# Layer 0's softmax-attention gate: weights stationary, a pair of row tiles moving

## The chip, the cores and the metric

The kernel runs on one core of a Trainium2 chip, in one launch. The core has TensorE (PE, with its weight loads shown apart as PEld), VectorE (DVE), ScalarE (ACT), GpSimd (POOL) and SyncE (SP, which issues DMAs). The metric is the device time of the kernel in microseconds (us), lower is better, as a median over several runs.

## The reference

A flow-matching backbone of two layers over 2304 tokens (256 of context, 2048 latent) of width 1024. Layer 0 mixes with multi-head latent attention and gated linear attention side by side, layer 1 with neighbourhood attention. Cut to the gate that the change concerns, which is `za` (512 features, `lat[3]` and `cp[3]`):

```
lat = split_cols(jnp.dot(h, w_in), EVEN_SPLITS)
...
a_x = block_attention(q_x, jnp.concatenate([k_x, k_c], axis=1), jnp.concatenate([v_x, v_c], axis=1), scale)
...
a = a.reshape(bsz, n, A_WIDTH) * jax.nn.silu(za)
b = rms_norm(b, gla_gain).reshape(bsz, n, B_WIDTH).astype(zb.dtype) * jax.nn.silu(zb)
return jnp.dot(jnp.concatenate([a, b], axis=-1), w_out)
```

`h` is the normed and modulated input of the layer, `zb` the like gate of the linear attention. SiLU is computed as (tanh(z/2) + 1) * z, a factor of 2 being taken care of elsewhere.

## The kernel before

Tokens are cut into 18 row tiles (NT) of 128 (P); the width of 1024 into 8 chunks (KD) of 128. Each float32 product is made of three matmuls over rounded halves: high by high, high by low and low by high (`mm3_steps`, lines L129, L130 and L131).

The stage concerned is `even_rest`. It projects the part of layer 0's input projection that is left over, 2080 columns in five pieces (`REST`): j = 0 is the gate `za` (512 columns, its weights called WU), j = 1 the gate `zb` (512, wr1), and j = 2, 3, 4 are three pieces of 352 (W0, W1, W2) for the linear attention. One `cell(t, j)` makes one piece for one row tile: 24 matmuls with a token tile (hhi or hlo, 128 x 128) stationary and the weights moving, into one of two PSUM banks called gm; tokens come out on the partitions. Both gates then take a tanh on ACT and a multiply on DVE (L632) into u, whose result POOL's queue sends to a scratch in DRAM. The gate `za` is wanted with its features on the partitions, since the attention reads it that way (`azt`, L966); so with j = 0 TensorE also transposes u in four blocks of 128 x 128 (L638) into a PSUM bank of its own, tp, ACT copies that to zt, and POOL sends zt to `zaT` (L641).

`stream` walks the cells in an order made by `cells`: per row tile the pieces 2, 3, 4, 0, 1, with two tiles taken together at either end. Pieces 2 and 3 of tiles 16 and 17 are made elsewhere, so there are 86 cells. It holds two token tiles (`hbufs`); after a tile's last cell `reload` fetches another: a DMA on SP's queue into x (one buffer), an ACT copy that makes hhi and a DVE subtraction that makes hlo.

`weave` puts a second sequence in between, `maxes`: for each of 8 heads it makes the scores of all queries (matmuls of 96 x 512, some of 96 x 256, into one of five PSUM banks mx, L665), of which DVE takes the row maximum (L666). At a head's end `post` transposes the 18 columns of maxima (L675), ACT copies them (mr), and POOL sends them into the queries' scratch (QT, L678). Besides, `weave` splits weights ahead of their use (`pump`), wr1 among them: a DMA into wraw, an ACT copy (L106 is the helper of all ACT work) and a DVE subtraction (L387).

Behind the stage comes `even_attention`. It first sets one row of each of four key buffers to one (memsets of akh on POOL, L910), loads queries and keys, and makes scores (st, L1016 to L1018) whose exponentials ACT takes (apt). Loading ACT's table for them is L1043.

Each engine takes its instructions in the order in which a scheduler has put them when the program is built; the order written in the code is where it starts from.

Of the kernel before, what the change touches and what calls it, by code (L numbers as in the profile page):

```python
# [11 lines left out]
F32R = mybir.dt.float32r  # L12
AF = mybir.ActivationFunctionType
ALU = mybir.AluOpType
# [3 lines left out]
P = 128  # L18
D = 1024
KD = D // P  # L20
# [3 lines left out]
NT = T // P  # L24
# [64 lines left out]
class Kern:  # L89
# [86 lines left out]
    def cells(tiles, js, keep=lambda t, j: True, edge=2):  # L176
# [2 lines left out]
        groups = [tiles[:edge]] + [[t] for t in tiles[edge : n - edge]] + [tiles[n - edge :]]  # L179
        return [(t, j) for g in groups for j in js for t in g if keep(t, j)]  # L180

    def stream(self, cells, hT, cell, prep, done=None):

        last = {}
        for n, (t, j) in enumerate(cells):
            last["t", t] = last["j", j] = n
        tiles = list(dict.fromkeys(t for t, _ in cells))
        for t in tiles[: self.hbufs]:
            if t not in hT:
                hT[t] = prep(t)  # L190
        for n, (t, j) in enumerate(cells):
            yield from cell(t, j)
            if last["j", j] == n and done:
                done(j)
            if last["t", t] == n:
                i = tiles.index(t) + self.hbufs
                if i < len(tiles):
                    del hT[t]
                    hT[tiles[i]] = prep(tiles[i])

    def rpow(self, out, in_, mul, add):
# [112 lines left out]
    def prep_pool(self, es, name, side, bufs, wbufs):  # L314
        self.prp = self.pool(es, name, bufs=2, side=side, reuse_waits="tile")
        self.hbufs, self.wbufs = bufs, wbufs

    def prep(self, l, t, src, pp, tag):

        return self.modulate(l, t, *self.transposed(t, src, pp, tag))  # L320

    def transposed(self, t, src, pp, tag, xp=None):

        nc, sp = self.nc, self.prp
        x = self.tl(xp or sp, [P, D], "x", bufs=1)
# [4 lines left out]
        self.act(lo[:].rearrange("p k t -> p (k t)"), x[:], AF.Square, accum_out=ss[:, 0:1])  # L330
# [21 lines left out]
    def reload(self, l, t):  # L352

        nc, sp = self.nc, self.prp
        x = self.tl(sp, [P, D], "x", bufs=1)
        nc.sync.dma_start(x[:], self.H[l, t])
        h = x[:].rearrange("p (k t) -> p k t", k=KD)
        hi = self.tl(sp, [P, KD, P], "hhi", F32R, bufs=self.hbufs)
        lo = self.tl(sp, [P, KD, P], "hlo", F32R, bufs=self.hbufs)
        self.act(hi[:], h)  # L360
        nc.vector.tensor_tensor(out=lo[:], in0=h, in1=hi[:], op=ALU.subtract)
        return hi, lo

    def split_w(self, *a, **kw):
# [248 lines left out]
    def even_rest(self, ws, win, hT):  # L613
        nc = self.nc
        self.zaT = self.scr("zaT", (4, P, T), F32)
        with ExitStack() as es:
            wp = self.pool(es, "ewB", side="left", reuse_waits="tile")
            sp = self.pool(es, "esB", bufs=2, side="left", reuse_waits="tile")
            pp = self.pool(es, "epB", bufs=2, space=PSUM, reuse_waits="tile")
            self.ahead += [self.rest_steps(win, 0, ws, "WU"), self.rest_steps(win, 1, wp, "wr1")]  # L620

            def cell(t, j):
                hi, lo = hT[t]
# [6 lines left out]
                if j < 2:  # L630
                    self.last_tanh = self.act(u[:], ps[:], AF.Tanh, scale=0.5)
                    nc.vector.scalar_tensor_tensor(out=u[:], in0=u[:], scalar=1.0, in1=ps[:], op0=ALU.add, op1=ALU.mult)  # L632
                else:
                    self.act(u[:, :w], ps[:, :w])
                if j == 0:
                    pt = self.tl(pp, [P, 4, P], "tp", bufs=1)
                    for b in range(4):
                        nc.tensor.transpose(pt[:, b, :], u[:, b * P : b * P + P], self.ident[:])  # L638
# [3 lines left out]
                elif j == 1:  # L642
                    nc.gpsimd.dma_start(self.Un[t, :, 1056:], u[:])
                else:
                    nc.gpsimd.dma_start(self.Un[t, :, (j - 2) * 352 : (j - 1) * 352], u[:, :352])

            cells = self.cells(list(range(NT))[::-1], (2, 3, 4, 0, 1), lambda t, j: j not in (2, 3) or t < NT - 2)
            gemms = self.stream(cells, hT, cell, lambda t: self.reload(0, t))

            def maxes():  # L650
                post = None
                for h in range(A_HEADS):
                    k = self.tl(sp, [P, T], "mk", F32R, bufs=2)
                    nc.sync.dma_start(k[:A_QK].bitcast(F32), self.KT[h, 0, :A_QK])
                    m = self.tl(sp, [P, NT, 5], "mm")
                    nc.vector.memset(m[:], -3e38)
                    for t in range(NT):
                        if t % 6 == 0:
                            q = self.tl(sp, [P, 768], "mq", F32R)
                            nc.sync.dma_start(q[:A_QK].bitcast(F32), self.QT[h, 0, :A_QK, t * P : t * P + 768])  # L660
                        lim = CTX if t < NCT else T
                        for n, k0 in enumerate(range(0, lim, 512)):
                            w = min(512, lim - k0)
                            ps = self.tl(pp, [P, 512], "mx", bufs=5)
                            mm = nc.tensor.matmul(ps[:, :w], q[:A_QK, (t % 6) * P : (t % 6) * P + P], k[:A_QK, k0 : k0 + w], start=True, stop=True)  # L665
                            nc.vector.tensor_reduce(out=m[:, t, n : n + 1], in_=ps[:, :w], axis=AX.X, op=ALU.max)  # L666
                            yield mm
                        if t == 3 and post:
                            yield post()
                    mc = self.tl(sp, [P, NT], "mc", bufs=1)  # L670
                    nc.vector.tensor_reduce(out=mc[:], in_=m[:], axis=AX.X, op=ALU.max)

                    def post(h=h, mc=mc):
                        ps = self.tl(pp, [P, 512], "mx", bufs=5)
                        mm = nc.tensor.transpose(ps[:NT, :P], mc[:], self.ident[:])  # L675
                        r = self.tl(sp, [P, P], "mr", F32R, bufs=1)
                        self.act(r[:NT], ps[:NT, :P], AF.Copy, scale=-1.0)
                        nc.gpsimd.dma_start(self.QT[h, 0, A_QK].rearrange("(t p) -> t p", p=P), r[:NT].bitcast(F32))  # L678
# [673 lines left out]
    def gate(self, out, in_):  # L1352

        self.last_tanh = self.act(out[:], in_, AF.Tanh, scale=0.5)
        self.nc.vector.scalar_tensor_tensor(out=out[:], in0=out[:], scalar=1.0, in1=in_, op0=ALU.add, op1=ALU.mult)
# [526 lines left out]
```

## Time and profile before

| | |
|---|---|
| runs shown | 3616.67, 3619.09, 3619.68 us; median 3619.09 |
| the profiled execution: own time | 3617.2 us |
| its span | 3615.4 us |
| the gate stage's steady part in the trace | 561.56 to 1083.06 us |

The span is what the profiler saw of the program's instructions; the own time has what lies around it. Views of the trace name a group as line, operation and tiles: `gm<-wr1h,hhi` is a matmul that writes gm from wr1's high half and a token tile's high half. Shapes stand as partitions x elements. "idle before" with an arrow says how long the engine stood before the instruction, and what released it.

### The profile page before, as it was taken

The page shows a single profiled execution, that of the slowest core. Times are in us where ns is not written, and L with a number is a line of the kernel's source. Part 1 is how long each engine was busy: PE and PEld are TensorE (multiplying, and loading weights), DVE is VectorE, ACT ScalarE, POOL GpSimd, SP SyncE. Part 2 cuts the span into 40 slices and gives each one's busy share as a digit, 9 for nine tenths or more (in the row PEclk, how much of TensorE's full clock was granted, in tenths as well). Part 3 has the DMA queues.
Part 4 walks back from the last instruction along what each step waited for, and adds up shares of the span by engine and source line. Part 5 has one row for each costly group of instructions (what it writes and reads, how often), then busy time and mean ns, then how long its engine had stood idle before and what let it go on. Part 6 is the DMA issues. An engine that isn't in the chain of part 4 may idle for free. (4 is left out here: it accounts for less than half of the span.)

```text
span 3615.4 us, 51630 instructions
## 1 busy us (share of the span) xinstructions
PE 3523.6 (97%) x18260; PEld 2734.3 (76%) x18260; DVE 2372.3 (66%) x4876; ACT 1430.5 (40%) x2705; POOL 1212.6 (34%) x1342
## 2 busy tenths in 40 slices
PE   8999999999999999999999999999999999999899
PEld 6988998888886666656667878888788886555577
DVE  4677665888886776787664345444587874667721
ACT  5544551111115555555653134444422223555510
POOL 1433430111011232212312233333334444677743
PEclk9999999999999999999999999999999999999999
DMA  7555463222233343334534544456643437888654
GB/s 253 149 153 159 141 191 99 87 77 84 75 109 89 83 104 83 94 92 129 163 91 143 162 164 127 145 143 199 212 139 123 139 122 202 213 213 222 185 178 146
DMA packets 396683, 513.62 MB, mean 142 GB/s; under 512 B 61229, under 2 KB 275197, under 8 KB 390522
## 3 DMA queue, kind: packets, MB, share of 16 engines
q1 hardware_dynamic: 353242, 418.68, 40.0%
q0 software_dynamic: 20192, 56.97, 5.6%
q10 hardware_dynamic: 22992, 34.68, 2.8%
q8 instruction: 145, 2.38, 0.3%
q14 instruction: 112, 0.92, 0.1%
HBM read 330.61 MB, written 179.59 MB: 141 GB/s over the span
## 5 line engine op out<-in xcount | busy, mean ns | idle before, releaser
L1007 DVE TENSOR_TENSOR acc<-acc,apt 128x512 f32<-128x512 f32 x512 | 376.4, 764 | 150.6 <-ACT apt L106 147.0
L666 DVE TENSOR_REDUCE mm<-mx 128x1 f32<-128x512 f32 (+1 forms) x656 | 392.7, 627 | 90.6 <-PE mx L665 82.3
L106 ACT ACTIVATE apt<-st 128x512 f32<-128x512 f32 (+1 forms) x592 | 342.9, 593 | 269.0 <-PE st L1018 229.5
L958 PE MATMUL av<-apt,av 128*64 128x512 f32 (+1 forms) x1184 | 269.2, 592 | 0.0
L1016 PE MATMUL st<-aq,akh 97*128 97x512 f32 x576 | 246.8, 428 | 0.2 <-ACT apt L106 0.2
L665 PE MATMUL mx<-mk,mq 96*128 96x512 f32 (+1 forms) x656 | 238.5, 372 | 0.0
L1017 PE MATMUL st<-aq,akh 96*128 96x512 f32 x576 | 229.1, 398 | 0.0
L1018 PE MATMUL st<-aq,akl 96*128 96x512 f32 x576 | 228.5, 397 | 0.0
L1450 DVE CUSTOM_DVE_ANT_1 mx<-mx,mtab 128x465 f32<-128x465 f32 (+14 forms) x576 | 183.9, 338 | 47.2 <-PE mx L1444 34.5
L106 ACT ACTIVATE u<-gm 128x352 f32<-128x352 f32 (+1 forms) x144 | 70.3, 495 | 358.5 <-PE gm L131 207.7
L106 ACT ACTIVATE opt<-opt 128x930 f32<-128x930 f32 (+9 forms) x144 | 119.2, 830 | 234.5 <-POOL opt L1748 137.0
L958 PEld LDWEIGHTS av<-apt,av 128*64 128x64 f32 x1184 | 79.9, 137 | 152.0 <-issue 150.0
L1708 DVE TENSOR_TENSOR opt<-st,tab 128x64 f32<-128x64 f32 (+10 forms) x576 | 143.0, 314 | 78.3 <-PE st L1548 44.7
L1583 POOL TENSOR_TENSOR oacc<-oacc,opt 128x682 f32<-128x682 f32 (+9 forms) x144 | 173.9, 1230 | 37.8 <-ACT opt L106 36.6
L1016 PEld LDWEIGHTS st<-aq,akh 97*128 97x128 f32 x576 | 109.0, 189 | 72.7 <-issue 44.2
L665 PEld LDWEIGHTS mx<-mk,mq 96*128 96x128 f32 x656 | 122.7, 188 | 11.7
L1018 PEld LDWEIGHTS st<-aq,akl 96*128 96x128 f32 x576 | 110.2, 191 | 25.5
L1017 PEld LDWEIGHTS st<-aq,akh 96*128 96x128 f32 x576 | 110.6, 192 | 17.8
L106 ACT ACTIVATE x<-px,modB,modA 128x128 f32<-128x128 f32 x272 | 99.1, 468 | 58.5 <-PE px L335 39.5
L1547 PE MATMUL st<-q,kt 128*128 128x480 f32 (+5 forms) x256 | 98.7, 388 | 20.2 <-DVE opt L1708 14.8
L129 PE MATMUL gm<-w0h,hhi 128*128 128x512 f32 x288 | 115.3, 400 | 2.3 <-DVE hhi L347 2.3
L129 PE MATMUL gm<-w1h,hhi 128*128 128x512 f32 x288 | 116.7, 405 | 0.0
(584 smaller groups left out, 9906.5 us busy)
## 6 DMA issues: line engine op xcount, KB each, us to landing
q<-Q SPq DMA_DIRECT2D x48, 512.0 KB
H<-x ACTq DMA_DIRECT2D x36, 512.0 KB
adaw<-ada_w SPq DMA_DIRECT2D x64, 256.0 KB
x<-H SPq DMA_DIRECT2D x32, 512.0 KB
K1t<-okt POOLq DMA_DIRECT2D x32, 512.0 KB, 6.7
kt<-K1t SPq DMA_DIRECT2D x32, 512.0 KB
mtab<-rpb_q SPq DMA_DIRECT2D x16, 899.0 KB
QT<-qkhl SPq DMA_DIRECT2D x36, 384.0 KB
```

The costliest lines, as they stand in the source:

```text
L106: return self.nc.scalar.activation(out, in_, func, **kw)
L129: self.nc.tensor.matmul(out, lh(k), rh(k), start=j == 0, stop=False)
L665: mm = nc.tensor.matmul(ps[:, :w], q[:A_QK, (t % 6) * P : (t % 6) * P + P], k[:A_QK, k0 : k0 + w], start=True, stop=True)
L666: nc.vector.tensor_reduce(out=m[:, t, n : n + 1], in_=ps[:, :w], axis=AX.X, op=ALU.max)
L958: nc.tensor.matmul(O[j, nb][i * 64 : i * 64 + 64, :w], V[j, kt // TT][:, kt % TT, i * 64 : i * 64 + 64], pts[i][:, :w], start=n == 0, stop ...
L1007: self.add = nc.vector.tensor_tensor(out=acc[i][:, :w], in0=a[:, :w], in1=pts[i][:, :w], op=ALU.add)
L1016: nc.tensor.matmul(ps[:, :w], kh[: A_QK + 1, i, kq], qh[: A_QK + 1, :w], start=True, stop=False)
L1017: nc.tensor.matmul(ps[:, :w], kh[:A_QK, i, kq], ql[:A_QK, :w], start=False, stop=False)
L1018: mm = nc.tensor.matmul(ps[:, :w], kl[:A_QK, i, kq], qh[:A_QK, :w], start=False, stop=True)
L1450: nc.vector.tensor_tensor_reduce(out=s, in0=s, in1=tb[:, ri : ri + rn, ci : ci + cn], scale=1.0, scalar=-3e38, op0=ALU.add, op1=ALU.max, a ...
L1583: self.psum = nc.gpsimd.tensor_tensor(out=a, in0=a, in1=pts[:, :, a0 - r0 : a1 - r0, :], op=ALU.add)
L1708: nc.vector.tensor_tensor(out=pt[:, d[0], d[1]], in0=ps[:, d[0], d[1]], in1=tabs[j][i][:, ri : ri + rn, ci : ci + cn], op=ALU.add)
```

## The change

The gate `za` is made for a pair of row tiles at once by `pair_steps`. Stationary is a slice of 128 of the weights' columns, that is 128 features; moving are the two tiles side by side, 256 tokens. To lay them side by side, the two token tiles now sit in one ring tile per half, `[P, bufs, KD, P]`, and a tile's place in it is `t % hbufs` (`slots`). A pair makes two blocks; each fills one gm bank with two groups of 128 features by 256 tokens, in 48 matmuls, with a step of the weave after each 6. The features come out on the partitions, tanh and multiply run on the block as it is, and POOL sends u to `zaT` without a transpose. There are 864 matmuls of 256 columns where there were 432 of 512; the columns streamed are the same. The 72 transposes, the 18 ACT copies and the bank tp are gone; mx has six banks in place of five. The multiplies and the sends to `zaT` stay 18 each.

The order of cells is written out: for a pair (t, t + 1) the pieces 2, 3, 4, 1 of tile t + 1, the gate of both, then 2, 3, 4, 1 of tile t, with the first and last pair apart.

```
+    def pair_steps(self, ps, blk, w):
+        hi, lo = self.ring
+        wh, wl = w
+        for n in range(2):
+            c = slice((blk + n) * P, (blk + n) * P + P)
+            o = ps[:, n * 256 : n * 256 + 256].rearrange("p (a t) -> p a t", a=2)
+            for j, k in enumerate(range(KD)):
+                self.nc.tensor.matmul(o, wh(k)[:, c], hi[:, :, k, :], start=j == 0, stop=False)
+                self.nc.tensor.matmul(o, wh(k)[:, c], lo[:, :, k, :], start=False, stop=False)
+                mm = self.nc.tensor.matmul(o, wl(k)[:, c], hi[:, :, k, :], start=False, stop=j == KD - 1)
+                if j % 2:
+                    yield mm
...
+        self.ring = [self.tl(self.prp, [P, bufs, KD, P], "h" + z, F32R, bufs=1) for z in ("hi", "lo")]
+    def slots(self, t):
+        return [r[:, t % self.hbufs] for r in self.ring]
...
-        hi = self.tl(sp, [P, KD, P], "hhi", F32R, bufs=self.hbufs)
-        lo = self.tl(sp, [P, KD, P], "hlo", F32R, bufs=self.hbufs)
+        hi, lo = self.slots(t)
...
+            def gated(t, j):
+                wh, wl = win[j]
+                for b in (0, 2):
+                    ps = self.tl(pp, [P, 512], "gm")
+                    yield from self.pair_steps(ps, b, (lambda k: wh[:, k, :], lambda k: wl[:, k, :]))
+                    u = self.tl(sp, [P, 512], "u", bufs=4)
+                    gate(u, ps)
+                    nc.gpsimd.dma_start(self.zaT[b : b + 2, :, t[0] * P : t[0] * P + 256].rearrange("j p t -> p j t"),
+                                        u[:].rearrange("p (j t) -> p j t", j=2))
...
-                if j == 0:
-                    pt = self.tl(pp, [P, 4, P], "tp", bufs=1)
-                    for b in range(4):
-                        nc.tensor.transpose(pt[:, b, :], u[:, b * P : b * P + P], self.ident[:])
-                    z = self.tl(sp, [P, 4, P], "zt")
-                    self.act(z[:], pt[:])
-                    nc.gpsimd.dma_start(self.zaT[:, :, t * P : t * P + P].rearrange("j p t -> p j t"), z[:])
...
+            cells = []
+            for t in range(NT - 2, -1, -2):
+                both = (t, t + 1)
+                if t == NT - 2:
+                    cells += [(t + 1, 4), (t, 4), (both, 0), (t + 1, 1), (t, 1)]
+                elif t == 0:
+                    cells += [(x, j) for j in (2, 3, 4) for x in (1, 0)] + [(both, 0), (1, 1), (0, 1)]
                 else:
-            cells = self.cells(list(range(NT))[::-1], (2, 3, 4, 0, 1), lambda t, j: j not in (2, 3) or t < NT - 2)
+                    cells += [(t + 1, j) for j in (2, 3, 4, 1)] + [(both, 0)] + [(t, j) for j in (2, 3, 4, 1)]
...
-                            ps = self.tl(pp, [P, 512], "mx", bufs=5)
+                            ps = self.tl(pp, [P, 512], "mx", bufs=6)
```

`stream` is taught that a cell may belong to two tiles. Lines of the changed program are shifted: the three matmuls of `pair_steps` are L190, L191 and L192, the maxima's matmuls L699, their transpose L709 and its send L712, the memsets L944, the first scores L1050.

On PE, in the middle of the stage, the transposes of a gate cell stand between the matmuls of the wr1 cell that follows (numbers behind a name count buffers). Before:

```order
L129 MATMUL gm_6485<-wr1h_5766,hhi_5963 128x512
L130 MATMUL gm_6485<-wr1l_5767,hhi_5963 128x512
L638 MATMUL tp_6477<-ident_58,u_6474 128x128 x2
L665 MATMUL mx_6332<-mk_5847,mq_6207 128x256
L638 MATMUL tp_6477<-ident_58,u_6474 128x128
L665 MATMUL mx_6338<-mk_5847,mq_6207 128x512
L638 MATMUL tp_6477<-ident_58,u_6474 128x128
```

With the change the gate's matmuls are 256 wide, and name the ring tile first and the weights second:

```order
L190 MATMUL gm_6262<-hhi_87,WUh_5658 128x256
L191 MATMUL gm_6262<-hlo_88,WUh_5658 128x256
L699 MATMUL mx_6228<-mk_5847,mq_6205 128x512
L192 MATMUL gm_6262<-hhi_87,WUl_5659 128x256
L190 MATMUL gm_6262<-hhi_87,WUh_5658 128x256
L191 MATMUL gm_6262<-hlo_88,WUh_5658 128x256
L699 MATMUL mx_6237<-mk_5847,mq_6205 128x256
L192 MATMUL gm_6262<-hhi_87,WUl_5659 128x256
```

No transposes are left there; score matmuls stand between the narrow ones as they stood between the wide ones.

On PE, at the end of the stage, the last head's maxima are transposed shortly before the last wr1 matmuls and the first scores. Before:

```order
L665 MATMUL mx_10352<-mk_9808,mq_10166 128x256
L129 MATMUL gm_10456<-wr1h_5766,hhi_10015 128x512
L130 MATMUL gm_10456<-wr1l_5767,hhi_10015 128x512
L131 MATMUL gm_10456<-wr1h_5766,hlo_10016 128x512
L675 MATMUL mx_10360<-ident_58,mc_10358 18x128
L129 MATMUL gm_10456<-wr1h_5766,hhi_10015 128x512
L130 MATMUL gm_10456<-wr1l_5767,hhi_10015 128x512
L131 MATMUL gm_10456<-wr1h_5766,hlo_10016 128x512
L1016 MATMUL st_12158<-aqc_10517,akh_1874_10509 128x256
```

With the change, from the same transpose (L709) on; the three rows from L130 to L129 stand there four times in all before two more follow:

```order
L129 MATMUL gm_10696<-wr1h_5744,hhi_87 128x512
L709 MATMUL mx_10575<-ident_58,mc_10573 18x128
L130 MATMUL gm_10696<-wr1l_5745,hhi_87 128x512
L131 MATMUL gm_10696<-wr1h_5744,hlo_88 128x512
L129 MATMUL gm_10696<-wr1h_5744,hhi_87 128x512
L130 MATMUL gm_10696<-wr1l_5745,hhi_87 128x512
L131 MATMUL gm_10696<-wr1h_5744,hlo_88 128x512
L129 MATMUL gm_10696<-wr1h_5744,hhi_87 128x512
```

Behind the transpose stood 3 wr1 matmuls, and now 14 stand there ahead of the first score matmul.

On POOL, at the same place, with what each instruction waits for, the order stays: the send of the maxima, then the memsets. With the change:

```order
L712 DMA QT<-mr_10577 18x128 [waits DMASW4_49,Activation_49]
L944 MEMSET akh_1772_10749 1x1536 [waits PE_49,Pool_49]
L944 MEMSET akh_1773_10750 1x1536
L944 MEMSET akh_1774_10751 1x1536
L944 MEMSET akh_1775_10752 1x1536 [waits PE_49]
```

Before, the same five stood there as L678 and L910; the memsets come behind the send on POOL, and so behind the maxima's copy on ACT. Moved is only the place of the transpose on PE that this send goes back to.

More of the change, by code (lines that the diff above doesn't have):

```diff
@@ L194, in stream @@
                 done(j)
[L195 to L198, printed above, removed]
+            for x in of(t):
+                i = tiles.index(x) + self.hbufs
+                if last["t", x] == n and i < len(tiles):
+                    del hT[x]
                     hT[tiles[i]] = prep(tiles[i])
@@ L357, in reload @@
         h = x[:].rearrange("p (k t) -> p k t", k=KD)
[L358 to L361, printed above, removed]
+        hi, lo = self.slots(t)
+        self.act(hi, h)
+        nc.vector.tensor_tensor(out=lo, in0=h, in1=hi, op=ALU.subtract)
         return hi, lo
@@ L673, in post @@
                     def post(h=h, mc=mc):
-                        ps = self.tl(pp, [P, 512], "mx", bufs=5)
+                        ps = self.tl(pp, [P, 512], "mx", bufs=6)
                         mm = nc.tensor.transpose(ps[:NT, :P], mc[:], self.ident[:])
```

26 lines of the change are left out of this document (16 added, 10 removed).

## The prediction

> **What bounds the kernel now.** I read the totals first, then the chain of waits, then the stage that the change touches.
>
> ```profile
> span 3615.4 us, 51630 instructions
> PE 3523.6 (97%) x18260; PEld 2734.3 (76%) x18260; DVE 2372.3 (66%) x4876; ACT 1430.5 (40%) x2705; POOL 1212.6 (34%) x1342
> PE 40%; DVE 2%; DMA 1%; issue 1%; ACT 1%; POOL 0%; SPq 0%; POOLq 0%; DVEq 0%; ACTq 0%
> ```
>
> TensorE is busy for 97% of the span, and the chain of work that ended last runs over it and hardly over anything else. The next view cuts out the gate stage (its steady part, then its end), the stretch behind it, and one later stretch for comparison. The columns are: stretch, length, busy time of PE, PEld, DVE, ACT and POOL, granted clock, DMA share, GB/s.
>
> ```profile
> core 0: us, PE busy (x) PEld busy (x) DVE busy (x) ACT busy (x) POOL busy (x), PEclk, DMA share, GB/s
> 561.56:1083.06 521.50, 521.40 (x2700) 462.07 (x2698) 429.61 (x721) 69.67 (x123) 52.51 (x90) 1.00 0.28 84
> 1083.06:1086.26 3.20, 1.32 (x10) 1.14 (x9) 0.69 (x1) 1.88 (x3) 3.11 (x3) 1.00 0.57 148
> 1086.69:1093.40 6.71, 6.71 (x17) 5.42 (x18) 1.54 (x3) 3.22 (x7) 3.15 (x5) 0.51 1.07 244
> 2872.70:2876.00 3.30, 3.04 (x15) 2.41 (x16) 3.30 (x13) 1.82 (x3) 0.26 (x1) 1.00 0.70 238
> ```
>
> In the steady part PE is busy 521.40 of 521.50 us at full clock: every matmul microsecond added or taken away there is a microsecond of the kernel. DVE is second with 429.61 (82%). ACT and POOL have far more room (70 and 53). At the end of the stage PE works 1.32 of 3.20 us, and behind it runs at half the clock.
>
> **Transposes that go.** The matmul timeline around one gate cell's transposes (start, length, then what; lengths overlap, so I read differences of starts):
>
> ```profile
> 727.12 0.39 PE L129 MATMUL gm<-wr1h,hhi 128*128 128x512 f32 x1
> ...
> 728.74 0.60 PE L638 MATMUL tp<-ident,u 128*128 128x128 f32 x4
> 729.10 0.48 PE L665 MATMUL mx<-mk,mq 96*128 96x512 f32 x1
> 729.42 0.40 PE L129 MATMUL gm<-wr1h,hhi 128*128 128x512 f32 x1
> L638 PE MATMUL tp<-ident,u x72: 270/272/475, 560.8 to 1073.5; 128*128 128x128 f32 x72
> ```
>
> Seven 512-wide matmuls take 727.12 to 728.74, 1.62 us, so 0.2314 each, with a weight load between each two. The four transposes take 0.36, and the matmul behind them 0.32 instead of 0.23: 0.45 us for one tile. There are 72 transposes, so 18 such groups: 18 x 0.45 = **-8.1 us**. The 18 ACT copies out of tp and their PSUM bank go too; ACT has room, so that is worth nothing, and a sixth mx bank is no gain where PE never waits.
>
> **Width.** The gate had 18 tiles x 8 chunks x 3 = 432 matmuls of 512 columns. Now there are 9 pairs x 4 feature groups x 8 x 3 = 864 of 256: the same columns, with 432 more weight loads. No pair of 128-row tiles ran that way before, so I look for 256-wide matmuls that each follow a load of their own. The nearest are the score matmuls right behind the stage, and around them the ends:
>
> ```profile
> 1085.34 0.28 PE L1017 MATMUL st<-aqc,akh 96*128 96x256 f32 x1
> 1085.46 0.28 PE L1016 MATMUL st<-aqc,akh 97*128 97x256 f32 x1
> 1085.46 0.19 PEld L1017 LDWEIGHTS st<-aqc,akh 96*128 96x128 f32 x1
> 1085.94 0.52 PE L1018 MATMUL st<-aqc,akl 96*128 96x256 f32 x3
> ...
> 2603.32 0.40 PE L1437 MATMUL mx<-mk,mz 128*128 128x256 f32 x2
> 2603.55 0.40 PE L131 MATMUL gm<-w0h,hlo 128*128 128x512 f32 x1
> ...
> 1081.16 0.29 PE L665 MATMUL mx<-mk,mq 96*128 96x256 f32 x1
> 1081.29 0.39 PE L129 MATMUL gm<-wr1h,hhi 128*128 128x512 f32 x1
> ...
> 1155.14 1.06 PE L791 MATMUL gl<-gu,gat 128*128 128x128 f32 x8
> 1155.95 0.47 PE L1017 MATMUL st<-aq,akh 96*128 96x512 f32 x1
> ```
>
> From 1085.34 to 1085.94 five steps take 0.60, so 0.120 each, though the load record alone is 0.19: loads run under the matmul ahead. The low end is the pair at 2603.32, 0.23 for two (0.115); the high end the lone one at 1081.16, 0.13. I take 0.120, since it is the row with a new weight at each step. 864 x 0.120 = 103.7 against 432 x 0.2314 = 100.0: **+3.7 us** (at 0.115 it is -0.6, at 0.13 it is +12.3). Eight 128-wide matmuls, each with its load, pass in 0.81, 0.101 each; below that a load could not be hidden, and 256 columns stay above it.
>
> [...]
>
> **The start of the stage.** Its first gate cell's ending is held up by weight splitting:
>
> ```profile
> 557.83 1.06 ACT L106 ACTIVATE wr1h<-wraw 128x1024 fp32r<-128x1024 f32 x1 [12.28 <-DMA wraw<-w_rest]
> 558.79 0.58 ACT L106 ACTIVATE u<-gm 128x512 f32<-128x512 f32 x1
> 560.06 0.68 DVE L632 SCALAR_TENSOR_TENSOR u<-u,gm 128x512 f32<-128x512 f32 x1
> 560.79 1.12 PE L638 MATMUL tp<-ident,u 128*128 128x128 f32 x4 [4.33 <-DVE u L632]
> 561.56 0.78 PE L129 MATMUL gm<-wr1h,hhi 128*128 128x512 f32 x1
> ```
>
> ACT stands at the split of a wr1 piece until its DMA lands; the tanh waits behind it, the multiply (L632) behind that, and PE waits 4.33 us. Without transposes the next PE work is the wr1 cell, which needs a gm bank that the same multiply gives back and the same wr1 pieces. So the stall stays: 0 (at best -0.8, the 0.77 us of these transposes, of which 0.45 is counted above).
>
> **The end of the stage.** What lies around the last matmul:
>
> ```profile
> 1082.24 0.28 PE L675 MATMUL mx<-ident,mc 128*18 128x128 f32 x1
> 1082.83 0.40 PE L131 MATMUL gm<-wr1h,hlo 128*128 128x512 f32 x1
> 1083.12 0.53 POOL L678 DMA_DIRECT2D QT<-mr  x1 [5.07 <-PE gm L130]
> 1083.32 0.60 ACT L106 ACTIVATE u<-gm 128x512 f32<-128x512 f32 x1 [0.49 <-PE gm L131]
> 1083.68 4.00 POOL L910 MEMSET akh<- 1x1536 f32 x3
> 1083.93 1.28 ACT L1043 ACT_TABLE_LOAD   x1
> 1085.11 0.39 PE L1016 MATMUL st<-aqc,akh 97*128 97x256 f32 x1 [1.88 <-POOL akh L910]
> 1086.26 0.38 ACT L106 ACTIVATE apt<-st 128x256 f32<-128x256 f32 x1 [1.04 <-PE st L1018]
> ```
>
> The last head's maxima are transposed (L675), copied, and sent by POOL; behind that issue stand POOL's memsets, and the first of them (4.00/3 = 1.33 us) holds the first score matmul for 1.88 us. From L675 to that memset's end it is 1083.68 + 1.33 - 1082.24 = 2.77 us. In the new order 14 wide matmuls follow that transpose instead of 3: 14 x 0.2314 = 3.24 us, so the memset is done before PE is, and PE may start 1085.11 - 1083.06 = 2.05 earlier. Late next is ACT: its tanh (1083.32) and the table load end at 1085.21, and no exponential can start before, where now it starts at 1086.26. **-1.0 us** (ends 0 and -2.05). Should the max's ending come late again, the 1.0 is lost.
>
> **The slow clock behind it.**
>
> ```profile
> 1087.50 0.63 PE L1016 MATMUL st<-aq,akh 97*128 97x512 f32 x1
> 1093.40 0.39 PE L1018 MATMUL st<-aq,akl 96*128 96x512 f32 x1
> ...
> 2872.70 0.66 PE L1395 MATMUL tp<-ident,ovz 128*128 128x128 f32 x4 [1.66 <-DVE ovz L1355]
> ```
>
> Fourteen matmuls take 1087.50 to 1093.40, 5.90 us, against 14 x 0.2314 = 3.24 at full clock: 2.66 lost. PE had idled 1.88 and soon after 1086.69 - 1086.26 = 0.43. In the new order PE works on until its score banks are full and waits for ACT, by my count 1.3 us. After an idle of 1.66 us (2872.70) the window above shows clock 1.00. I take **-2.7** (the other end is 0, the drop stays).
>
> [...]
>
> **Covers.** DVE's multiplies keep their number; the 18 sends to zaT also. The cell order now runs four or five cells of one token tile in a row, and the other tile's reload (a copy, a subtraction and a DMA) has to be done before the pair cell. The 86 cells of the old order share some 521 us, 6.1 each with the maxima between them, so four cells give 24 us; a reload is a DMA, and a copy and a subtraction of the size of the wr1 rows above (1.06 and 1.22), so it is hidden. Uncovered, it would show as PE waiting for DVE at L191 for each pair.
>
> **Sum**, against the profiled execution (span 3615.4, 3617.2 with what lies around it): -8.1 + 3.7 - 1.0 - 2.7 = -8.1, so 3609.1. The median of the runs shown lies 1.9 above it, at 3619.09: forecast **3611**.
>
> **Rivals.**
>
> *The load sets the pitch of a narrow matmul* (slower). In a long run of 256-wide matmuls the loads could fail to keep ahead: the record of one is 0.19. Then 864 x 0.19 = 164.2, +64.2 - 11.8 (the other three terms) = +52, some 3671. It decides from a pitch of 0.125 on, where width (108.0 - 100.0) eats the transposes; at 0.133 the whole is nil. For it: five steps are a short chain, and PEld's work in this stage grows from 462 by 432 x 0.19 = 82 to 544, beyond 521. Against it: records overlap, and the 0.101 of eight in a row. Chance 0.15.
>
> *The end term or the clock does not come*: the idle keeps its length, the clock falls as it did, and transposes less width remain, -4.4, 3615: within what can be told from no change. For it: my count of 1.3 us idle lies close to the 1.88 that went wrong. Chance 0.22.
>
> *DVE becomes the bound in bursts.* DVE has 82% now, and a stretch where maxima (one per wide score matmul) come close together can make PE wait for an mx bank. If each of 18 gate ends costs 0.3, less than half of an L632 multiply of 0.68, 5.4 us go, -2.7 in all, 3616. Against it: six banks instead of five. Chance 0.08.
>
> *The change does not overlap as written*: the pair cell waits for both tiles, and one reload is late in each of 9 pairs by more than 0.9 us: no gain, 3619 or more. Chance 0.05.
>
> **The numbers.** The forecast has 0.50. What a measurement of this kernel can tell from no change is about 0.2%, 7.2 us, so the forecast is just beyond that border, and its own range (pitch 0.115 to 0.125, end and clock as bounded) is 3606 to 3616; so I give 0.37 of its 0.50 to faster and 0.13 to the same. The second rival gives 0.06 to faster (at a pitch of 0.115), 0.14 to the same and 0.02 to slower; DVE's bursts 0.06 to the same and 0.02 to slower; the reload 0.02 and 0.03; the load's pitch 0.15 to slower. Together faster 0.43, same 0.35, slower 0.22. For 8 in 10 the range leaves out the 0.19 pitch and runs from 3603 (the low ends of all terms, with a little below them) to 3624 (a pitch of 0.13 with neither the end's gain nor the clock's).
>
> **What would show it.** Right: 864 matmuls on L190 to L192 about 0.12 apart, no transposes to tp, PE busy over 99.5% of the stage, the stage shorter by about 4 us; the first score matmul right behind the last gate matmul and clock 1.00 there. Wrong: pitch of 0.125 or more, PE waits at L190 to L192 for DVE or at the gm bank, or again 0.5 for the clock behind the stage.

## The result, and the profile after

| | before | changed |
|---|---|---|
| median of 20 runs each | 3619.68 us | 3611.99 us |
| lowest and highest | 3610.3, 3627.44 | 3600.39, 3617.17 |
| ratio to before, 95% interval | | 0.9975 [0.9967, 0.9983] |
| profiled execution: span | 3615.4 | 3611.7 |

The ratio is a gain of 0.0025 x 3619.68 = 9.0 us (6.2 to 11.9); 8.1 were forecast, to 3611. The one profiled pair differs by only 3.7 us, for a reason that has nothing to do with the gate (last section), so from here on I read stretches, not spans.

The page of the changed kernel, its totals and its chain:

```profile
span 3611.7 us, 52299 instructions
PE 3522.7 (98%) x18620; PEld 2751.5 (76%) x18620; DVE 2375.7 (66%) x4876; ACT 1420.3 (39%) x2687; POOL 1210.8 (34%) x1342
PE 41%; DVE 2%; DMA 1%; issue 1%; ACT 1%; POOL 0%; SPq 0%; POOLq 0%; DVEq 0%; ACTq 0%
```

360 matmuls more (432 more in the gate, 72 transposes fewer), and TensorE still bounds. The windows over the wait ahead of the steady part, the steady part, its end and the stretch behind it (length, busy time of PE, PEld, DVE, ACT, POOL, granted clock, DMA share, GB/s):

```profile
556.68:559.26 2.58, 0.05 (x1) 0.00 (x1) 1.88 (x3) 2.58 (x4) 0.00 (x0) 1.00 0.02 6
559.26:1076.20 516.94, 516.94 (x3016) 475.03 (x3016) 428.31 (x721) 58.89 (x106) 54.36 (x93) 1.00 0.28 85
1076.43:1079.02 2.59, 1.24 (x10) 1.03 (x8) 0.69 (x1) 2.31 (x4) 2.59 (x3) 1.00 0.44 84
1079.48:1082.98 3.50, 3.50 (x17) 2.85 (x16) 1.42 (x3) 2.71 (x6) 1.17 (x4) 1.00 1.07 268
```

From the first wr1 matmul to the last, PE is busy all of 516.94 us, where it took 521.27 before (1082.83 - 561.56). Behind the stage the clock is 1.00 where it was 0.51. The first pair of gate cells and the wait behind it (timeline: start, length, engine):

```profile
545.21 0.28 PE L190 MATMUL gm<-hhi,WUh 128*128 128x256 f32 x1
...
556.29 1.06 ACT L106 ACTIVATE wr1h<-wraw 128x1024 fp32r<-128x1024 f32 x1 [10.42 <-DMA wraw<-w_rest]
556.45 0.28 PE L192 MATMUL gm<-hhi,WUl 128*128 128x256 f32 x1
557.25 0.58 ACT L106 ACTIVATE u<-gm 128x512 f32<-128x512 f32 x1
...
558.52 0.68 DVE L653 SCALAR_TENSOR_TENSOR u<-u,gm 128x512 f32<-128x512 f32 x1
559.26 0.79 PE L129 MATMUL gm<-wr1h,hhi 128*128 128x512 f32 x1 [2.53 <-DVE u L653]
```

Its 96 matmuls start 545.21 to 556.45: 11.24 / 95 = 0.118 each. The wait for the multiply is still there, behind the same wr1 split. The end of the stage:

```profile
1073.05 0.27 PE L709 MATMUL mx<-ident,mc 128*18 128x128 f32 x1
...
1073.91 0.53 POOL L712 DMA_DIRECT2D QT<-mr  x1 [0.77 <-ACT mr L106]
...
1074.48 5.33 POOL L944 MEMSET akh<- 1x1536 f32 x4
...
1076.20 0.39 PE L131 MATMUL gm<-wr1h,hlo 128*128 128x512 f32 x1
1076.43 0.28 PE L1050 MATMUL st<-aqc,akh 97*128 97x256 f32 x1
...
1077.29 1.28 ACT L1077 ACT_TABLE_LOAD   x1
...
1078.59 0.94 ACT L106 ACTIVATE apt<-st 128x256 f32<-128x256 f32 x3
1079.02 0.39 PE L1050 MATMUL st<-aqc,akh 97*128 97x256 f32 x1 [1.35 <-ACT apt L106]
...
1079.48 0.40 PE L1050 MATMUL st<-aq,akh 97*128 97x512 f32 x1
```

The first score matmul follows the last gate matmul at once. What PE waits for now is ACT's first exponential, which waits for the table load: 1.35 us of idle, and no slow clock after it.

One difference lies far from the gate: at the program's end POOL runs a DRAIN. It is the longest of three on its line (shortest, median and longest in ns, then where they start), before and changed:

```profile
L1876 POOLq DRAIN  x3: 40/102/7275, 3607.4 to 3615.2; - x3
L1910 POOLq DRAIN  x3: 40/93/4990, 3606.0 to 3611.5; - x3
```

The other engines wait for a semaphore of POOL's behind this drain before the program ends: the drain ends at 3610.95 us and their last steps start at 3611.1, before at 3614.64 and 3614.8. It takes 4.99 us instead of 7.28: 2.3 us that no term of the forecast has. From the start of the last matmul to the end of the span it is 9.3 us in the four profiles of kernels with the old gate (before, e1, e2, e7), and 7.0 or 7.1 in the seven with the new one. Why the drain is shorter was not followed.

The table has three stretches, worked out from the starts of the same matmuls in each profile: **first** from the first gate matmul to the first wr1 matmul; **steady** from there to the stage's last matmul; **end** from there to the sixteenth 512-wide score matmul.

| kernel | first | steady | end | sum | ratio to before |
|---|---|---|---|---|---|
| before | 16.68 | 521.27 | 10.80 | 548.75 | |
| changed | 14.05 | 516.94 | 6.79 | 537.78 | 0.9975 [0.9967, 0.9983] |
| changed, again (e11) | 15.61 | 516.92 | 6.79 | 539.32 | 0.9969 [0.9956, 0.9982] |
| no transposes (e1) | 16.51 | 513.99 | 9.39 | 539.89 | 0.9967 [0.9955, 0.9979] |
| before, maxima earlier (e2) | 17.88 | 520.05 | 6.77 | 544.70 | 0.9994 [0.9984, 1.0004] |
| changed, five banks (e4) | 16.74 | 517.85 | 10.82 | 545.40 | 0.9990 [0.9982, 0.9999] |
| five banks, maxima earlier (e10) | 16.29 | 516.04 | 6.77 | 539.11 | 0.9960 [0.9947, 0.9974] |
| 128 columns moving (e6) | 21.39 | 595.49 | 8.32 | 625.19 | one run, 3719.14 us |
| before, new cell order (e7) | 16.75 | 521.36 | 10.76 | 548.86 | 0.9995 [0.9983, 1.0007] |
| changed, keys behind wr1 (e8) | 15.60 | 516.86 | 6.79 | 539.24 | 0.9998 [0.9989, 1.0007] |
| changed, tanh first (e9) | 11.37 | 515.27 | 6.79 | 533.43 | 0.9954 [0.9941, 0.9967] |

### The profile page after: what moved, and what is told of

Same layout as the page of the kernel before. It is cut to its first block, busy times and chain, and to the rows that moved or that the text cites. A ratio compares the mean times of both kernels' runs of the same rounds, so it can differ in the third digit from the quotient of the medians.

```text
span 3611.7 us, 52299 instructions
## 1 busy us (share of the span) xinstructions
PE 3522.7 (98%) x18620; PEld 2751.5 (76%) x18620; DVE 2375.7 (66%) x4876; ACT 1420.3 (39%) x2687; POOL 1210.8 (34%) x1342
## 5 line engine op out<-in xcount | busy, mean ns | idle before, releaser
L1050 PE MATMUL st<-aq,akh 97*128 97x512 f32 x576 | 246.1, 427 | 0.2 <-ACT apt L106 0.2
L699 PE MATMUL mx<-mk,mq 96*128 96x512 f32 (+1 forms) x656 | 242.7, 372 | 0.0
L1050 PEld LDWEIGHTS st<-aq,akh 97*128 97x128 f32 x576 | 108.6, 188 | 72.4 <-issue 43.4
L699 PEld LDWEIGHTS mx<-mk,mq 96*128 96x128 f32 x656 | 123.7, 189 | 6.0
L129 PE MATMUL gm<-w0h,hhi 128*128 128x512 f32 x288 | 116.2, 403 | 2.3 <-DVE hhi L367 2.3
L129 PE MATMUL gm<-w1h,hhi 128*128 128x512 f32 x288 | 116.5, 404 | 0.0
```

Of the source, the lines that this page charges most:

```text
L129: self.nc.tensor.matmul(out, lh(k), rh(k), start=j == 0, stop=False)
L1050: nc.tensor.matmul(ps[:, :w], kh[: A_QK + 1, i, kq], qh[: A_QK + 1, :w], start=True, stop=False)
```

## Experiments

**e1: the transposes alone.** In the kernel before:

```
-                    pt = self.tl(pp, [P, 4, P], "tp", bufs=1)
-                    for b in range(4):
-                        nc.tensor.transpose(pt[:, b, :], u[:, b * P : b * P + P], self.ident[:])
-                    z = self.tl(sp, [P, 4, P], "zt")
-                    self.act(z[:], pt[:])
-                    nc.gpsimd.dma_start(self.zaT[:, :, t * P : t * P + P].rearrange("j p t -> p j t"), z[:])
+                    nc.gpsimd.dma_start(self.zaT[:, :, t * P : t * P + P].rearrange("j p t -> p j t"), u[:].rearrange("p (j t) -> p j t", j=4))
```

> The kernel before, with the 72 transposes and their 18 copies left out: u is sent to the scratch as it is, so this kernel's gate values stand in the wrong places, with the same bytes sent. Theory: the transposes cost PE 18 x 0.39 to 0.45 in the steady part and 0.8 in the slow stretch at its start, 7 to 8 us in all, and nothing else moves: ratio to before 0.9978 to 0.9981, the steady part about 7 us shorter than before's, the first score matmul still waiting for the memset. Rival one: the whole gain of the change is the transposes plus what they entangle, 9 us or more (ratio under 0.9976). Rival two: transposes were hidden, under 2 us.

Measured: 0.9967 [0.9955, 0.9979]. The steady window of e1, and that of before:

```profile
557.74:1071.73 513.99, 513.89 (x2629) 455.79 (x2630) 429.87 (x721) 59.23 (x106) 52.53 (x90) 1.00 0.28 85
```

```profile
561.56:1082.83 521.27, 521.17 (x2699) 462.07 (x2698) 429.61 (x721) 69.67 (x123) 52.51 (x90) 1.00 0.28 84
```

7.28 us less. 68 of the 72 transposes start in this stretch, 17 of the 18 groups: 0.43 each. So the first theory's steady part holds. The first group stands in the first stretch: from the start of the wr1 split that holds the tanh up to the first wr1 matmul it is 557.83 to 561.56 before, 3.73, and 2.96 in e1, so the 0.8 came too, though the split itself started 0.6 later there. The changed kernel's steady part is 516.94 - 513.99 = 2.95 longer than e1's: that is the price of the width, with 0.24 in it for two of the maxima's matmuls, 256 wide, that stand in the first stretch in e1. The ratio reads 12 us, more than the theory, and by the ratio alone rival one would stand; the three stretches give 8.9 of it. 1.4 of the 8.9 are at the end, where the slow clock was shorter (last section); the other 3 us of the 12 lie outside the stage, where nothing was changed, and the interval allows 8.

**e6: what sets the pitch of a narrow matmul.** One tile moving at a time:

```
+            for a in range(2):
+                for j, k in enumerate(range(KD)):
+                    self.nc.tensor.matmul(o[:, a, :], wh(k)[:, c], hi[:, a, k, :], start=j == 0, stop=False)
...
```

> The changed kernel with each gate matmul cut in two: one tile of 128 tokens moving, 1728 matmuls of 128 columns, each with a load of its own. Theory: with 256 columns the pitch is set by the columns (0.119 each, 512 take 0.231), and with 128 it is set by the load, at the 0.101 of the transposes: 1728 x 0.101 = 174.5 against 102.7 now, the gate's matmuls 72 us longer. Rival: the load's own record of 0.19 is the floor: 328 us, 225 longer. Other rival: the load hides altogether and the columns decide: 0.06 each, no change.

Measured: 3719.14 us in one run. Two rows of the timeline, with 14 matmuls of the same kind between them:

```profile
547.74 0.27 PE L193 MATMUL gm<-hhi,WUl 128*128 128x128 f32 x1
...
549.41 0.27 PE L193 MATMUL gm<-hhi,WUl 128*128 128x128 f32 x1
```

15 steps take 1.67: 0.111 each, where 256 columns take 0.118 and 512 take 0.231. Halving the columns from 512 to 256 halves the pitch within 3%; halving them again saves almost nothing. So 256 columns lie just above a floor for this form: 128 columns, with a load at each step, took 0.111 where half of 0.118 would be 0.059. It is not the load's record of 0.19. Nor is it the 0.101 that I took from eight 128-wide matmuls, which were L791's and no transposes, as the expectation has it: their row's 1.06 us less one matmul's 0.28 is 0.78 for seven steps, 0.111 each. I had divided by eight up to the next matmul, which starts only 0.03 behind the last. The gate's matmuls become 1728 x 0.111 - 864 x 0.118 = 90 us longer, and the table's sum grows by 87. The profile's further 18 us lie behind the stage, nearly all of them between 1170 and 1790 us, where the attention was scheduled in another order; some 5 of them are a slower clock, and the rest was not followed.

**e2 and e4: the end of the stage, put on and taken off.** e2 is the kernel before with `self.weave(gemms, maxes(), 1.06, 30, 28)`, e4 the changed kernel with `bufs=5` for mx.

> The kernel before, with the maxima started 4 weave steps earlier (head 28 instead of 32), so that 15 wide matmuls instead of 3 stand between the last transpose of maxima and the first score matmul; nothing else is changed. Theory: the end term alone, 1.0 us from the first exponential and 2.7 us from a clock that does not fall, -3.7 us in all (ratio 0.9990), and in the profile the first score matmul right behind the last gate matmul. Rival: the clock falls wherever its window happens to lie, so an idle of 1.3 us does not save it, and only -1.0 comes. Other rival: what is gained there is waited for later, 0.

> The changed kernel with five banks for the maxima instead of six. The scheduler then puts the last transpose of maxima 3 wide matmuls ahead of the first score matmul again, not 14. Theory: in the steady part nothing changes (within 0.5 us), and at the end the memset is late again and the clock falls: 3.7 us slower than the changed kernel, about 0.9983 to 0.9990 of before. Rival: the sixth bank matters in the steady part, with PE waiting at the maxima's matmuls for DVE: more than 5 us slower than the changed kernel. Other rival: the end term is chance, no difference.

Measured: e2 0.9994 [0.9984, 1.0004], e4 0.9990 [0.9982, 0.9999]. The end of the stage in e2:

```profile
1081.99 4.01 POOL L910 MEMSET akh<- 1x1536 f32 x3
...
1082.60 0.39 PE L131 MATMUL gm<-wr1h,hlo 128*128 128x512 f32 x1
1082.83 0.28 PE L1016 MATMUL st<-aqc,akh 97*128 97x256 f32 x1
...
1084.99 0.94 ACT L106 ACTIVATE apt<-st 128x256 f32<-128x256 f32 x3
...
1085.43 0.38 PE L1016 MATMUL st<-aqc,akh 97*128 97x256 f32 x1 [1.36 <-ACT apt L106]
```

and in e4:

```profile
1075.87 0.40 PE L131 MATMUL gm<-wr1h,hlo 128*128 128x512 f32 x1
...
1076.73 4.00 POOL L944 MEMSET akh<- 1x1536 f32 x3
...
1078.15 0.39 PE L1050 MATMUL st<-aqc,akh 97*128 97x256 f32 x1 [1.89 <-POOL akh L944]
```

with this window behind it (clock 0.50):

```profile
1079.55:1086.40 6.85, 6.66 (x17) 5.41 (x18) 1.54 (x3) 3.36 (x8) 3.34 (x5) 0.50 1.07 262
```

In e2, four weave steps bring the memsets ahead of the last gate matmul, and the end takes 6.77 instead of 10.80: -4.03, though no gate is touched (its first wr1 matmul stands somewhat later in the order; first and steady together are before's, 537.93 and 537.95). In e4, one bank less puts the transpose of the maxima back to 3 matmuls before the scores, and the end is 10.82 again. So the end term comes and goes with the order alone, the gate left as it is; how much of it the clock gives is another matter (last section). e4's steady part is 0.9 longer than the changed kernel's, outside the 0.5 expected: behind a wait of 5.21 us the clock was 0.50 up to 564.14, for 6.1 us of the steady part instead of 3.4. In the runs e4 lies 0.0015 above the changed kernel, 5 us with intervals that just touch; in e2 the 4 us are inside the interval but do not stand clear of nothing.

**e10: is the sixth bank worth anything itself?** Five banks, and `head` 28:

> The changed kernel with five banks for the maxima, and these started 4 weave steps earlier (head 28), so that 15 wide matmuls stand between their last transpose and the first score matmul as in the changed kernel (14). Theory: what five banks cost was their effect on the order at the end, so the end term comes back whole: first score matmul right behind the last gate matmul, first exponential 2.4 us after it, clock 1.00, and the time is the changed kernel's within 1.5 us. Rival: the sixth bank is worth something in the steady part, which then stays 1 us or more longer than the changed kernel's 516.9.

Measured: 0.9960 [0.9947, 0.9974]. Its steady window, and the one behind the stage:

```profile
563.47:1079.51 516.04, 515.79 (x3011) 473.96 (x3012) 431.13 (x721) 59.25 (x106) 54.72 (x93) 1.00 0.28 85
...
1082.70:1086.30 3.60, 3.60 (x19) 2.95 (x18) 1.43 (x3) 2.83 (x6) 1.04 (x4) 1.00 1.07 280
```

The steady part is no longer than with six banks, and the end is whole. By the ratios e10 lies 3 us below the changed kernel's repetition (0.9969), more than the 1.5 expected, with intervals that overlap. The sixth bank helped the changed kernel only by what it did to the scheduler's order.

**e7: the order of cells alone**, in the kernel before:

> The kernel before with the changed kernel's order of cells alone (the two tiles' gate cells behind one another in each pair), gates still made and transposed tile by tile. Theory: the order is worth nothing, within 1 us of before, the same idle and clock at the end. Rival: part of the gain comes from the order, since reloads and sends are spread otherwise: -2 us or more. Other rival: the order costs, because a reload is late: +2 us or more.

Measured: 0.9995 [0.9983, 1.0007], and all three stretches as before to within 0.1 us. The order of cells is worth nothing.

**e8: the wait at the start, first try.** The next head's keys are loaded by a helper that, for the second head, is ordered behind the last weight load. The edit also changes a second line, which the expectation does not name, in the linear attention that runs between the scores behind the stage: there an order between small matmuls (L816 in the changed kernel, L824 in e8) is replaced:

```
+                def keys(h):
+                    ks[h] = k = self.tl(sp, [P, T], "mk", F32R, bufs=2)
+                    with self.tc.issue_after(self.wload.ins) if h == 1 else ExitStack():
+                        nc.sync.dma_start(k[:A_QK].bitcast(F32), self.KT[h, 0, :A_QK])
...
-                    with self.tc.issue_after(mm.ins) if mm else ExitStack():
+                    with self.tc.issue_after(self.wload.ins) if h == 1 else ExitStack():
                         mm = nc.tensor.matmul(two[z][:, h * P : h * P + P], kT[z * 64 : z * 64 + 64, h, :], qT[z * 64 : z * 64 + 64, h, :],
```

> The changed kernel with the load of the second head's keys (864 KB) ordered behind the last two pieces of wr1 on SP's queue, instead of ahead of them. Theory: PE's wait of 2.5 us in the first gate cells' ending is made by the DMA of those pieces, on which ACT stands with the tanh queued behind it; 864 KB at some 270 GB/s are 3.2 us, so the pieces land that much sooner, the wait goes, and with it the slow clock right behind it (3.5 us at 0.52, 1.6 us): 2.5 to 4 us faster than the changed kernel, ratio to before 0.9964 to 0.9968. Rival: the DMA queues share their bandwidth, so the order of issue moves the landing by less than 1 us and nothing is gained. Other rival: the keys come late for the second head and PE waits there.

Measured: 0.9998 [0.9989, 1.0007], a miss. ACT, DVE and PE in e8, where the first gate matmul is at 542.78:

```profile
552.72 1.06 ACT L106 ACTIVATE wr1h<-wraw 128x1024 fp32r<-128x1024 f32 x1 [9.27 <-DMA wraw<-w_rest]
...
555.41 1.06 ACT L106 ACTIVATE wr1h<-wraw 128x1024 fp32r<-128x1024 f32 x1 [1.64 <-DMA wraw<-w_rest]
556.38 1.06 ACT L106 ACTIVATE u<-gm 128x512 f32<-128x512 f32 x2
...
558.38 0.79 PE L129 MATMUL gm<-wr1h,hhi 128*128 128x512 f32 x1 [4.08 <-DVE u L653]
```

The same in the changed kernel's repetition (e11), where the first gate matmul is at 546.53:

```profile
559.18 1.06 ACT L106 ACTIVATE wr1h<-wraw 128x1024 fp32r<-128x1024 f32 x1 [11.98 <-DMA wraw<-w_rest]
560.14 0.58 ACT L106 ACTIVATE u<-gm 128x512 f32<-128x512 f32 x1
...
562.14 0.79 PE L129 MATMUL gm<-wr1h,hhi 128*128 128x512 f32 x1 [4.08 <-DVE u L653]
```

Counted from the first gate matmul, the third piece did land sooner (9.9 us after it instead of 12.7). But the scheduler now put both remaining pieces ahead of the first tanh, which comes 13.6 us after the first gate matmul in both, and PE waits 4.08 in both. So the theory that the DMA's landing makes the wait was half of it: what makes it is that the tanh stands in order behind a piece that is not there yet. The three stretches are those of e11, and yet e8's time is no better than before's. Some 10 us are lost between 1100 and 1600 us, and that is the second line of the edit. The changed kernel's row and e8's, in the same time:

```profile
1134.04 1.16 PE L816 MATMUL gl<-gqT,gkT 64*128 64x128 f32 x14
```

```profile
1133.74 1.16 PE L824 MATMUL gl<-gqT,gkT 64*128 64x128 f32 x8
```

14 matmuls pass in the changed kernel where 8 pass in e8. By the line that was replaced they alternated between the two halves of 64 rows, and they start in pairs, 0.007 and 0.105 us apart; in e8 many come 0.111 apart. From each one's start to the next matmul's, all 288 take 24.8 us in the changed kernel and 34.6 in e8: 9.8 more. So e8's time says nothing about the keys, only its first stretch does; no run has the keys' line alone.

**e9: the wait at the start, by its cause.** The third and fourth pieces' copies are ordered behind the first gate block's tanh; on ACT and on DVE one row changes places, on PE, SP and POOL none:

```
                 if rows is None:
-                    self.act(hi[:, s, c], w[:])
+                    with self.tc.issue_after(self.last_tanh.ins) if tag == "wr1" and k0 >= 4 else ExitStack():
+                        self.act(hi[:, s, c], w[:])
```

> The changed kernel with one swap on ACT and the same on DVE: the first gate block's tanh and multiply are put ahead of the third and fourth wr1 pieces, which are still loading. PE's order and SP's are unchanged. Theory: PE waited 2.5 us (5.2 in another profile, by when the pieces land) because the tanh stood in order behind a split that waits for its DMA; with the swap wr1's first 12 matmuls run while the pieces land, so the wait goes or shrinks below 1 us, and the slow clock behind it (1.6 us) with it: 3 to 5 us faster than the changed kernel, ratio to before 0.9961 to 0.9967. Rival: the pieces are late anyway and PE waits as long at wr1's fifth chunk: no difference. Other rival: the gain in the stage is lost to slow-clock windows in later stages.

> The changed kernel itself, on the same chip as the two others, so that they have it beside them. Theory: 0.9975 of before again, within 0.0008; first gate matmul to the sixteenth wide score matmul 537 to 541 us, by when wr1's pieces land.

Measured on one chip: e9 0.9954 [0.9941, 0.9967], the changed kernel again 0.9969 [0.9956, 0.9982]. ACT and PE in e9:

```profile
552.57 0.60 ACT L106 ACTIVATE u<-gm 128x512 f32<-128x512 f32 x1 [5.21 <-PE gm L192]
...
558.01 1.06 ACT L106 ACTIVATE wr1h<-wraw 128x1024 fp32r<-128x1024 f32 x1 [4.84 <-DMA wraw<-w_rest]
558.05 0.40 PE L129 MATMUL gm<-wr1h,hhi 128*128 128x512 f32 x1
...
559.48 1.06 ACT L106 ACTIVATE wr1h<-wraw 128x1024 fp32r<-128x1024 f32 x1 [0.41 <-DMA wraw<-w_rest]
```

The tanh runs as soon as its block is done, wr1's first matmul follows the last gate matmul at once, and the pieces land under it. The first stretch is 11.37 us, the 96 matmuls and nothing else, and the steady part loses 1.65 more, since no slow clock follows (the 512-wide matmuls from 558.05 on start 0.23 apart): 5.9 us less than e11 in all. That is a little over the 3 to 5 expected. In the runs it is 0.0015 of 3622, 5.4 us; the two intervals overlap, so the runs alone do not prove what the stretches show. e9 has the lowest ratio of all, and it is faster than before beyond doubt. The repetition came as expected, in its ratio and in its sum of 539.32.

## Why the prediction was right

**Transposes**, forecast -8.1: 0.43 for a group instead of 0.45, -7.3 for the 17 groups in the steady part (e1); the first group is counted with the start. Right.

**Width**, forecast +3.7 at a pitch of 0.120: the pitch is 0.118, so 864 x 0.118 - 100.0 = +2.0, and +2.95 by the difference of two profiles (e1 and the changed kernel), of which 0.24 belongs to the maxima. The row that was taken, 256-wide score matmuls each with a load of its own, was the right neighbour. The rival by which a load's record of 0.19 sets the pitch is refuted: PE took 0.118 with a load at each step, and PEld's work in the steady part grew to 475 us, not to the 544 that adding up records gave. But e6 shows that a floor was near, above the prediction's 0.101, which no run shows: at 128 columns the pitch is 0.111 and no longer follows the columns.

**The start**, forecast 0: the wait is still there, 2.53 and 4.08 us in two profiles and 5.21 in e4, against 4.33 before. How long it is depends on when wr1's pieces land. From the start of the split that holds the tanh to the first wr1 matmul, though, it is 2.97 and 2.96 in the two profiles of the changed kernel against 3.73 before: 0.8 is a gain, the transposes of the first group, which the forecast named as the end of this term and did not take. The first stretch is shorter by 2.6 us in the first profile and by 1.1 in the repetition; what is over 0.8 there is the pieces' landing. e9 shows the mechanism of the wait.

**The end**, forecast -1.0 and -2.7 for the clock: from the last gate matmul to the first exponential it is 1078.59 - 1076.20 = 2.39 instead of 1086.26 - 1082.83 = 3.43, that is -1.04; the whole end is 4.0 shorter, which leaves -3.0 for the clock. Both came, and e2 and e4 show them with the gate left alone. My count of 1.3 us of idle came out as 1.35. But the clock's part was in part luck: it came in six of seven profiles with this idle, and in five of the six a raster in time, which lies differently in each profile, had cut the idle in two (last section). Nor did the row that it leaned on bear it, an idle of 1.66 us with the clock at 1.00 behind it: at the same place of the changed kernel an idle of 1.44, shorter still, was followed by 0.50 (2866.68 to 2870.10). The second idle before, which the prediction put at 0.43 by an ACT row, was 0.24 for PE.

**The sum**: -7.3 + 2.95 - 0.8 - 4.0 = -9.1 against -8.1 forecast; the stretches give -9.4 (e11), with 0.3 of landing in it. With the closing drain, which was not forecast, it is -11.4. The runs say -9.0 (6.2 to 11.9) and allow both, so the near hit of the total is no proof that no term was missed: the drain's 2.3 was. Two figures of the prediction do not come out of its own terms: the change would be nil at a pitch of 0.129, not 0.133, and its own range would end at 3619, not 3616, with the pitch at 0.125 and neither the end's gain nor the clock's.

One step was right only by way of the order list: "a sixth mx bank is no gain where PE never waits". The bank itself is indeed worth nothing (e10), but it is what moved the transpose of the maxima, and with it 4 of the 9 us (e4). What is left to the new gate itself is -7.3 + 2.95 - 0.8 = -5.2 us, a little over half of the gain in the stretches.

DVE did not become a bound (428 of 517 us busy, PE never idle in the steady part), and no reload was late.

## What to carry to other kernels

Swapping the operands to spare a transpose paid here because the moving side stayed wide enough that the pitch still followed its columns (0.231 at 512, 0.118 at 256, but 0.111 at 128): find in a trace the narrowest matmul that has a load of its own at each step, and break even against that. When a change frees a bank or moves a step count, read the order of the engines at the stage's two ends too, for a few steps of order there were worth as much as the change (4.0 us at the end in e2, 5.9 in e9, against 5.2 for the gate itself). And when an engine that works in order stands at a split whose data is still loading, look at what is queued behind it: moving that ahead helped here, where loading earlier did not, as the scheduler then put the waiting work behind one more piece. And where one run changes two things, as e8 did, its time speaks for neither.

## What the runs showed of the hardware that was not expected

Behind this stage TensorE idles 1.35 or 1.36 us in seven of the profiles, and 1.9 and soon another 0.24 in the four others (before, e1, e4, e7). After the long idle the clock fell in all four. After the short one it stayed at 1.00 in six, and fell in one, e6. Two windows of 3.41 us, one with its idle and the next:

```profile
1163.11:1166.53 3.42, 2.06 (x12) 1.66 (x12) 1.54 (x3) 2.93 (x7) 2.25 (x5) 1.00 0.80 204
1166.53:1169.94 3.41, 3.41 (x10) 2.66 (x9) 0.69 (x1) 1.72 (x4) 0.00 (x0) 0.50 1.05 234
```

The traces say more than this count. In each of them the clock is 1.00 or 0.50 and nothing between, so any other value in a window is a mean; and all half-clock stretches but the one at the program's end start on one raster of 3.413 us. In the changed kernel those at 559.28 and 1562.79 us lie 294 steps apart, 1003.52 us. Where the raster falls on an idle differs from profile to profile. In five of the six that kept the clock (changed, e8 to e11), a step ended within the short idle and cut it, so that no step held more than 1.06 us of it. In e6, above, and in e2 one step held it whole:

```profile
1082.52:1085.93 3.41, 2.05 (x16) 1.76 (x15) 0.69 (x1) 2.82 (x5) 3.41 (x3) 1.00 0.47 111
1085.93:1089.34 3.41, 3.41 (x17) 2.80 (x16) 1.39 (x3) 2.65 (x5) 0.90 (x4) 1.00 1.07 274
```

PE was busy 2.05 us of that step in e2 and 2.06 in e6, and in the next step the clock was 1.00 in the one and 0.50 in the other. The long idle lay whole in one step before and in e4 and e7, and two steps at 0.50 came of it; in e1 it was cut in two, and one step came. So the rival in e2's expectation, that it depends on where a window of the clock happens to lie, is right in part: where the raster lies decides whether the idle is cut, and whole in one step 1.36 us came out either way. What else decides there was not settled.

The clock also scatters where nothing was changed. The same stretch of 20.48 us in layer 1, in the changed kernel and before:

```profile
3030.53:3051.01 20.48, 16.87 (x44) 11.16 (x46) 10.89 (x32) 9.17 (x16) 11.33 (x6) 0.50 1.08 263
```

```profile
3035.49:3055.97 20.48, 16.50 (x74) 10.29 (x75) 12.03 (x35) 9.38 (x17) 11.34 (x6) 0.83 1.08 275
```

The granted clock is 0.50 and 0.83, and 0.67 in the changed kernel's repetition. That is up to 0.33 x 20.48 = 6.8 us of full clock, but it is not time lost. From the first matmul behind the wait here to the same matmul 316 later, in the same two profiles:

```profile
3033.96:3089.59 55.63, 53.97 (x316) 35.16 (x317) 34.30 (x102) 27.49 (x45) 36.57 (x29) 0.85 0.95 233
```

```profile
3038.58:3094.18 55.60, 52.13 (x316) 33.87 (x317) 35.56 (x102) 27.35 (x45) 35.72 (x29) 0.91 0.95 233
```

Both take 55.6 us: before has two more half-clock steps a little later, and waits for a DMA there. What made the profiled pair differ by 3.7 us where the runs say 9.0 lies elsewhere: four half-clock steps behind the stage, at 1562.8, 2866.7, 3184.1 and 3231.9 us of the changed kernel, that before does not have at these places, 4 x 1.7 = 6.8 us. They are no mark of the new gate: e2 and e7, with the old one, have the first of them too. An effect of this size is better read from its own stretch than from two spans, and a clock only together with the time between the same two instructions.
